# Part of the opening of a layer trunk moved between VectorE and TensorE: two tiles' modulation, and the sums of squares

## The chip, the cores and the metric

The kernel runs on one core of one Trainium2 chip. A core has a matrix engine (TensorE, PE in the profile; its weight loads are listed apart as PEld), a vector engine (VectorE, DVE), an activation engine (ScalarE, ACT), GpSimd (POOL) and SyncE (SP), which here issues the DMAs. TensorE writes into PSUM, eight banks of 128 x 512 fp32; everything else works on the on-chip memory SBUF. The metric is the device time of one execution in microseconds (us); less is better. The kernel before took 2400.89 us (median of three runs, 2396.86 to 2404.48).

## What is computed

Two layers of a trunk, each with a token mixer and a gated ConvFFN, on one sequence of 1024 tokens with 1024 features. Ahead of each sub-layer stands an RMSNorm whose result is scaled and shifted by values that come from a conditioning vector `c`:

```python
cond = jax.nn.silu(c)
for i in range(DEPTH):
    mod = (cond @ ada_w[i] + ada_b[i])[:, None, :]
    sh1, sc1, g1, sh2, sc2, g2 = jnp.split(mod, 6, axis=-1)
    h = rms_norm(x, norm_g[i, 0]) * (1.0 + sc1) + sh1
    ...   # first mixer: z = gelu(h @ w_in), u and v are its halves
```

What matters here is the first few lines for layer 0: `sh1` and `sc1` (1024 values each, the product of `cond` with 1024 x 1024 weights each), the sum of squares of each token for the norm, and then the product of `h` with the `v` half of `w_in`.

## The kernel before

Features lie on the partitions: `xT` holds x as eight tiles (d = 0 to 7) of 128 features by 1024 tokens, in two halves of 512 tokens, LO and HI. The opening works on LO. Precise products are made of three reduced ones: each operand is split into a high and a low part, and `mm3` (L277, its matmul at L280) issues high x high, high x low and low x high.

The program is a list of operations that `Plan` (L108) orders. Each has an engine, a duration as the plan supposes it, the tiles it reads and writes, and a priority `pr`; `emit` lays them out by a small model of the engines, and what comes out is the order in which each engine runs its instructions. Each engine then runs that order strictly, waiting where an operand is not there.

The opening, L992 to L1085, goes like this:

- **Fillers.** `warm` (L966) multiplies a tile of ones by itself (128 columns) into a bank that nobody reads. 14 of them stand ahead of the first real work, 10 after the sums of squares, 8 after the norm's broadcast.
- **The condition.** `c` is loaded as one row (L994), behind three of the loads of x; TensorE spreads it over 128 partitions by a product with ones (L1004, two matmuls), ScalarE takes the sigmoid (L1006), VectorE multiplies (L1007). The row, now silu(c) on every partition, stays in `raw_2` for all later dot products.
- **The norm.** For each tile ScalarE squares (L454, L1016); VectorE adds seven of the squares into `accv` (L459); TensorE sums `accv` and the last square over partitions (L1020, four one-column matmuls each, with the squares as the stationary operand). VectorE takes the root (L314 to L324), puts it on a diagonal (L368), and TensorE spreads it over the partitions (L373).
- **The modulation.** The weights of `sc1` and `sh1` for tile d lie in DRAM with outputs on the partitions (128 outputs by 1024 inputs). VectorE makes a dot product with the row of silu(c) for each: `ada_dot` (L286), 1024 elements a partition. `ada_group` (L291) adds the bias (L296) and forms the gain (L300). The same operation, `first_values` (L1034), then writes the normed tile (L1042). ScalarE makes its high part (L487), VectorE its low part (L488).
- **The weights of v** (512 KB blocks, two feature tiles each) are split by ScalarE (L500) and VectorE (L503).
- **The products.** `first_mms` (L1049) multiplies each tile with two blocks for four groups of 128 tokens, 24 matmuls a tile into all eight banks. Tile 0's come in three groups of eight: high x high, then those with tile 0's low part, then those with the weights' low part.

SyncE issues the loads in the order of the plan (`p_load`, L514): x, then for each tile its two modulation blocks, with the blocks of v between, into ten buffers that are used in turn. A buffer is loaded anew when its last reader has finished.

Of the kernel before, what the change touches and what calls it, by code (L numbers as in the profile page):

```python
# [244 lines left out]
def trunk(tc, a, pool, psum, dram):  # L245
# [45 lines left out]
    def ada_group(l, w, d=0, n=KT, nw=1):  # L291
# [4 lines left out]
        V.tensor_tensor(out=v, in0=v, in1=cols(pc("ada_b", l * 48, 48)), op=ALU.add)  # L296
# [669 lines left out]
    def warm(n, w, pr, *preds):  # L966
        for _ in range(n):
            pl.op("PE", w, lambda: PE.matmul(bank[7][:, 0:P], ones, ones, start=True, stop=True), *preds,
                  r=(onesrg,), w=(bv(7),), pr=pr)
# [24 lines left out]
    pl.op("D", 0.1, lambda: nc.sync.dma_start(condr[0:1, :], a["crow"]), w=(rv(2),), pr=SB - 31)  # L994
# [15 lines left out]
    warm(10, 0.3, SB - 29)  # L1010


    ps0, sq, sqs3 = bv(6), sqs.v[3], Seq(*sqs.v[0:3])
    for d in range(KT - 1):
        p_sum(pl, nm0, d, accv, sqs3, SB - 3)
    pl.op("S", 0.63, lambda: S.activation(sq.f, xT[:, KT - 1, LO], AF.Square), r=(xrg(KT - 1, LO),), w=(sq,), pr=SB - 3)  # L1016
    for i, x in enumerate((sq, accv)):
        def fn(i=i, x=x):
            for c in range(4):
                PE.matmul(ps0.f[:, c:c + 1], x.f[:, c * P:(c + 1) * P], ones[:, 0:1], start=i == 0 and c == 0, stop=i == 1,  # L1020
                          skip_group_check=True)
        last = pl.op("PE", 0.9, fn, r=(x,), w=(ps0,), pr=SB - 3)
    warm(10, 0.22, SB - 40, last)
# [2 lines left out]
    def chain(ops=ops):
# [2 lines left out]
    pl.op("V", 1.95, chain, r=(ps0,), w=(("small0", 0, 16),), pr=SB - 3)
    after = pl.op("V", 0.63, lambda r0=r0: nm0.diag(r0), r=(("small0", 0, 16), params), w=(accv,), pr=SB - 3)  # L1030
# [1 line left out]
    warm(8, 0.22, SB - 40, last)

    def first_values(d, raws, *preds):  # L1034
# [3 lines left out]
        def fn():  # L1038
            for m, raw in raws:
                ada_dot((m, raw.f))  # L1040
            ada_group(0, 0, d, 1, 2)
            V.scalar_tensor_tensor(out=t.f, in0=xT[:, d, LO], scalar=amul[:, d:d + 1], in1=rb.f, op0=ALU.mult, op1=ALU.mult)  # L1042
# [973 lines left out]
```

## Time and profile before

| | |
|---|---|
| median of the runs | 2400.89 us |
| profiled execution, its time | 2402.39 us |
| its span | 2400.6 us |
| TensorE busy | 2370.1 us, 99% |
| VectorE busy | 2063.9 us, 86% |
| first product of the mixer (L280) | 20.82 us |
| products run on without a gap from | 26.55 us |
| granted TensorE clock, mean | 0.994 |

The span reaches from the first to the last instruction; the time beside it is that of the same execution with what lies around it. All that the change touches lies in the first 70 us, so the views of that stretch matter: the timeline of each engine, who waits for whom, and the granted clock, a share of TensorE's full rate. A row of a timeline gives start, duration, engine, line, operation, tiles, count, and in brackets the idle time ahead of it and what ended it. Each fp32 matmul leaves two records.

### The profile page before, as it was taken

To read this page: it belongs to the slowest core of one execution; us is meant where nothing else is said; L and a number is where in the kernel's file an instruction comes from. 1 tells how busy PE (TensorE), PEld (TensorE's weight loads), DVE (VectorE), ACT (ScalarE), POOL (GpSimd) and SP (SyncE) were. 2 spreads that over 40 slices of the span, in tenths; PEclk is the share of its full clock that TensorE was granted. 3 is DMA by queue.
4 is the path that set the end of the run, shared out by engine and by line. 5 is a ranking of instruction groups with operands and counts; after the bars stand their busy time and mean duration, and the time that the engine had idled before them with its cause. 6 is when DMAs were issued, how large, how long until landed. Compare 5 with 4: busy or idle time off the path is not lost.

```text
span 2400.6 us, 32858 instructions
## 1 busy us (share of the span) xinstructions
PE 2370.1 (99%) x11358; PEld 1976.7 (82%) x11358; DVE 2063.9 (86%) x3322; ACT 1288.8 (54%) x2301; POOL 449.9 (19%) x312
## 2 busy tenths in 40 slices
PE   9999999999999999999999999999999999999998
PEld 7888887788888888888788888888888888887886
DVE  8899988988989889998988788887689988898756
ACT  4546664455555555445566666665255555544444
POOL 0222110322222221012301111111122222220121
PEclk8999999999999999999999999999999999999999
DMA  9667769720333324865301111225313333338332
GB/s 338 194 217 255 238 205 308 258 81 27 123 96 121 113 92 143 296 218 180 122 15 52 45 45 45 71 62 157 105 42 110 104 117 108 107 123 285 95 104 97
DMA packets 154827, 330.91 MB, mean 138 GB/s; under 512 B 15522, under 2 KB 34338, under 8 KB 154660
## 3 DMA queue, kind: packets, MB, share of 16 engines
q1 hardware_dynamic: 154660, 328.81, 41.8%
q8 instruction: 89, 1.46, 0.3%
q14 instruction: 78, 0.64, 0.1%
HBM read 253.77 MB, written 74.98 MB: 137 GB/s over the span
## 4 chain that ended last, share of the span: by engine, by line
PE 93%; DVE 2%; DMA 2%; issue 1%; ACT 1%; POOL 0%; SPq 0%; POOLq 0%; ACTq 0%; DVEq 0%
PE pb L280 85%; PE pb L1626 4%; PE pb L1346 1%; PE pb L1691 1%; PE pb L1711 1%; DMA h<-act 0%; PE pb L1713 0%; DVE w L503 0%; DMA xT<-vd 0%; PE pb L373 0%; DVE h L503 0%; PE pb L1684 0%; PE pb L1734 0%; DMA h<-gact 0%; DMA w<-in_down 0%
## 5 line engine op out<-in xcount | busy, mean ns | idle before, releaser
L280 PE MATMUL pb<-h,w 128*128 128x512 f32 (+1 forms) x4470 | 1038.5, 388 | 8.5 <-ACT h L500 2.9
L280 PEld LDWEIGHTS pb<-h,w 128*128 128x128 f32 x4470 | 832.5, 188 | 184.8 <-ACT h L500 4.2
L280 PE MATMUL pb<-n,w 128*128 128x512 f32 x3312 | 790.1, 391 | 1.8 <-ACT wk L735 1.0
L280 PEld LDWEIGHTS pb<-n,w 128*128 128x128 f32 x3312 | 617.6, 188 | 130.7 <-ACT wk L735 1.5
L503 POOL TENSOR_TENSOR w<-w,w 128x512 fp32r<-128x512 f32 x170 | 260.5, 1537 | 952.2 <-ACT w L500 913.9
L500 ACT ACTIVATE w<-w 128x512 fp32r<-128x512 f32 x405 | 249.8, 627 | 265.4 <-PE pb L280 162.0
L893 DVE SCALAR_TENSOR_TENSOR raw<-wk,prm,raw 128x1024 f32<-128x1024 f32 x168 | 266.3, 1594 | 7.4 <-ACT raw L889 6.3
L503 DVE TENSOR_TENSOR w<-w,w 128x512 fp32r<-128x512 f32 x235 | 169.8, 728 | 32.6 <-ACT w L500 31.7
L500 ACT ACTIVATE w<-n 128x512 fp32r<-128x512 f32 x136 | 85.8, 631 | 163.8 <-PE pb L280 151.6
L735 ACT ACTIVATE wk<-pb 128x512 f32<-128x512 f32 x160 | 94.7, 593 | 139.9 <-PE pb L280 117.7
L280 PE MATMUL pb<-w,n 128*128 128x512 f32 x612 | 144.5, 397 | 3.6 <-DVE n L488 3.6
L738 DVE TENSOR_TENSOR wk<-pb,wk 128x512 f32<-128x512 f32 x160 | 108.3, 686 | 45.5 <-PE pb L280 40.8
L280 PEld LDWEIGHTS pb<-w,n 128*128 128x128 f32 x612 | 116.5, 191 | 29.8 <-DVE n L488 4.5
L503 POOL TENSOR_TENSOR w<-raw,w 128x512 fp32r<-128x512 f32 x55 | 78.5, 1440 | 328.6 <-ACT w L500 216.9
L503 DVE TENSOR_TENSOR w<-n,w 128x512 fp32r<-128x512 f32 x136 | 101.1, 746 | 44.5 <-ACT w L500 44.1
L500 ACT ACTIVATE h<-h 128x512 fp32r<-128x512 f32 x198 | 121.8, 618 | 25.1 <-DMA h<-gact 12.8
L889 ACT ACTIVATE raw<-wk,prm 128x1024 f32<-128x1024 f32 x84 | 103.6, 1240 | 32.8 <-DVE raw L510 12.9
L280 PE MATMUL pb<-w,h 128*128 128x512 f32 x480 | 116.9, 396 | 0.0
L503 DVE TENSOR_TENSOR h<-h,h 128x512 fp32r<-128x512 f32 x150 | 110.2, 739 | 6.9 <-ACT h L500 6.9
L503 POOL TENSOR_TENSOR h<-h,h 128x512 fp32r<-128x512 f32 x48 | 67.9, 1414 | 197.9 <-ACT h L500 186.2
L280 PEld LDWEIGHTS pb<-w,h 128*128 128x128 f32 x480 | 88.1, 188 | 17.4
L442 DVE SCALAR_TENSOR_TENSOR xT<-pb,mod,xT 128x512 f32<-128x512 f32 (+1 forms) x108 | 74.4, 727 | 24.5 <-PE pb L280 24.2
(278 smaller groups left out, 2927.9 us busy)
## 6 DMA issues: line engine op xcount, KB each, us to landing
w<-in_up SPq DMA_DIRECT2D x88, 512.0 KB, 3.7
act<-raw SPq DMA_DIRECT2D x154, 256.0 KB, 2.2
h<-act SPq DMA_DIRECT2D x124, 256.0 KB, 2.8
h<-in_ada SPq DMA_DIRECT2D x45, 512.0 KB, 4.7
wk<-in_ada SPq DMA_DIRECT2D x33, 512.0 KB, 4.6
n<-in_down SPq DMA_DIRECT2D x64, 256.0 KB, 5.4
gact<-xT SPq DMA_DIRECT2D x56, 256.0 KB, 3.8
h<-gact SPq DMA_DIRECT2D x56, 256.0 KB, 3.9
```

Of the source, the lines that this page charges most:

```text
L280: PE.matmul(ps, L[i // 2], R[i % 2], start=first and i == 0 and not more, stop=last and i == 2, skip_group_check=more)
L442: V.scalar_tensor_tensor(out=xT[:, d, hs], in0=ps.f, scalar=gate(d), in1=xT[:, d, hs], op0=ALU.mult, op1=ALU.add)
L500: pl.op("S", 0.2 + 0.43 * w, lambda: S.activation(hi.r, src.f, AF.Copy), r=(src,), w=(hi,), pr=pr)
L503: lambda: e.tensor_tensor(out=lo.r, in0=src.f, in1=hi.f, op=ALU.subtract), *preds,
L735: pl.op("S", 0.6, lambda: S.activation(c.f, ps.f, AF.Copy), r=(ps,), w=(c,), pr=p(i) - 10)
L738: pl.op("V", 0.69, lambda: V.tensor_tensor(out=c.f, in0=ps.f, in1=c.f, op=ALU.add), r=(ps, c), w=(c,), pr=p(i) - 8)
L889: pl.op("S", 1.22, lambda: S.activation(y.f, wk[:, o + PADW:o + PADW + T], AF.Identity, bias=pc("conv_b", l * NUP + b), scale=cw(2)), r=(c ...
L893: pl.op("V", 1.26, lambda w=w: V.scalar_tensor_tensor(out=y.f, in0=wk[:, o + w:o + w + T], scalar=cw(w), in1=y.f, op0=ALU.mult, op1=ALU.ad ...
L1346: PE.matmul(ps.f[:, i * P:(i + 1) * P], v.f[:, i * P:(i + 1) * P], wsT[:, j, :], start=True, stop=True)
L1626: PE.matmul(ps_()[0:m, c, :], K.f[:, c * P:c * P + m], q, start=True, stop=True)
L1691: PE.matmul(b2.f[:, cs(c)], kT.f[:, cs(c)], vc(c), start=True, stop=True)
L1711: PE.matmul(b3.f[:, cs(c)], sc.f[:, cs(c)], vc(c), start=True, stop=s_ is None)
```

## The change

Four things change, all in the opening.

- **Condition.** `c` is loaded twice, ahead of x: as a column (`ccol`, 128 x 8, element k of partition p is feature 128 k + p) and as the row of before. ScalarE and VectorE make silu of the column (`csl`).
- **Squares.** ScalarE squares all eight tiles, and TensorE sums each of them as it comes: four one-column matmuls a tile, 32 in all, into one accumulation. VectorE's adds are gone. Root and diagonal become one operation of the plan, and the splits of the first two blocks of v no longer wait for a tile's values.
- **Modulation of tiles 0 and 1** (`NPE = 2`). Their weights come from a copy with inputs on the partitions (`adaf`); `pe_dots` multiplies each 128 x 128 block, as the stationary operand, by one column of `csl`: eight matmuls for each of the two columns of a tile, into one column of bank 7 (tile 0) or 5 (tile 1). `ada_group` then reads the sums from PSUM. Tiles 2 to 7 stay with VectorE.
- **Fillers.** 7 in place of 14 ahead of the squares, 4 in place of 10 behind them, 4 in place of 8 behind the norm's broadcast; they write bank 3 instead of 7.

```diff
@@ ada_group
-    def ada_group(l, w, d=0, n=KT, nw=1):
+    def ada_group(l, w, d=0, n=KT, nw=1, ps=None):
...
-        V.tensor_tensor(out=v, in0=v, in1=cols(pc("ada_b", l * 48, 48)), op=ALU.add)
+        src = v if ps is None else ps.rearrange("p (w d) -> p w d", d=n)
+        V.tensor_tensor(out=v, in0=src, in1=cols(pc("ada_b", l * 48, 48)), op=ALU.add)
@@ the opening
-    pl.op("D", 0.1, lambda: nc.sync.dma_start(condr[0:1, :], a["crow"]), w=(rv(2),), pr=SB - 31)
+    cc, csig, csl = (cct[:, i * KT:i * KT + KT] for i in range(3))
+    ccrg = ("cc", 0, 1)
+
+    def load_cond():
+        nc.sync.dma_start(cc, a["ccol"])
+        nc.sync.dma_start(condr[0:1, :], a["crow"])
+    pl.op("D", 0.2, load_cond, w=(ccrg, rv(2)), pr=SB - 32)
+    pl.op("S", 0.25, lambda: S.activation(csig, cc, AF.Sigmoid), w=(ccrg,), pr=SB - 32)
+    pl.op("V", 0.17, lambda: V.tensor_tensor(out=csl, in0=cc, in1=csig, op=ALU.mult), w=(ccrg,), pr=SB - 32)
...
-    warm(10, 0.3, SB - 29)
+    warm(3, 0.3, SB - 29)
...
-    ps0, sq, sqs3 = bv(6), sqs.v[3], Seq(*sqs.v[0:3])
-    for d in range(KT - 1):
-        p_sum(pl, nm0, d, accv, sqs3, SB - 3)
-    pl.op("S", 0.63, lambda: S.activation(sq.f, xT[:, KT - 1, LO], AF.Square), r=(xrg(KT - 1, LO),), w=(sq,), pr=SB - 3)
-    for i, x in enumerate((sq, accv)):
-        def fn(i=i, x=x):
+    ps0, psd = bv(6), (bv(7), bv(5))
+    nm0.acc = accv.f
+    for d in range(KT):
+        q = sqs.next()
+        pl.op("S", 0.6, lambda d=d, q=q: S.activation(q.f, xT[:, d, LO], AF.Square), r=(xrg(d, LO),), w=(q,), pr=SB - 25 + d)
+
+        def fn(d=d, q=q):
             for c in range(4):
-                PE.matmul(ps0.f[:, c:c + 1], x.f[:, c * P:(c + 1) * P], ones[:, 0:1], start=i == 0 and c == 0, stop=i == 1,
-                          skip_group_check=True)
-        last = pl.op("PE", 0.9, fn, r=(x,), w=(ps0,), pr=SB - 3)
-    warm(10, 0.22, SB - 40, last)
+                PE.matmul(ps0.f[:, c:c + 1], q.f[:, c * P:(c + 1) * P], ones[:, 0:1], start=d == 0 and c == 0,
+                          stop=d == KT - 1, skip_group_check=True)
+        last = pl.op("PE", 0.7, fn, r=(q, onesrg), w=(ps0,), pr=SB - 25 + d)
+    warm(4, 0.22, SB - 40, last)
...
-    warm(8, 0.22, SB - 40, last)
+    warm(4, 0.22, SB - 40, last)
+
+    def pe_dots(d, raws):
+
+        for m, raw in raws:
+            def fn(raw=raw, col=m // KT):
+                for k in range(KT):
+                    PE.matmul(psd[d].f[:, col:col + 1], raw.f[:, k * P:k * P + P], csl[:, k:k + 1], start=k == 0, stop=k == KT - 1)
+            pl.op("PE", 1.2, fn, r=(raw, ccrg), w=(psd[d],), pr=SB - 2.5 + d)
@@ first_values
-            ada_group(0, 0, d, 1, 2)
+            ada_group(0, 0, d, 1, 2, psd[d].f[:, 0:2] if d < NPE else None)
@@ the loop over tiles and blocks
-            after = p_split(pl, x, *vset[p, q], "V", SB + nw - 1.4 if nw < 8 else SB + 9 + nw, ys[-1])
+            after = p_split(pl, x, *vset[p, q], "V", SB + nw - 1.4 if nw < 8 else SB + 9 + nw, ys[-1] if nw > 1 else None)
...
-            p_load(pl, x, a["ada"][0, m], pr)
-        if d == 0:
-            p_dot(*raws.pop(0), SB, after)
+            p_load(pl, x, a["adaf"][m // KT, d] if d < NPE else a["ada"][0, m], pr)
+        if d < NPE:
+            pe_dots(d, raws)
+            raws = []
@@ _lay_out
+    first = stat(f["ada_w"][0][:, :2 * D])
+    out["adaf"] = np.stack([first[0:NPE], first[KT:KT + NPE]])
+    out["ccol"] = cols(f["c"])
```

TensorE's order in the opening is the first place of which the prediction speaks. `pb_75` to `pb_82` are the banks 0 to 7, `h_...` and `w_...` are buffers with a version number, and each row is an instruction as the program has it (two records each in the profile). Before, from the start:

```order
L968 MATMUL pb_82<-ones 128x128 x14
L1004 MATMUL pb_79<-raw_67,ones 128x512
L1004 MATMUL pb_80<-raw_67,ones 128x512
L1020 MATMUL pb_81<-ones,wk 128x1 x8
L968 MATMUL pb_82<-ones 128x128 x10
L373 MATMUL pb_81<-wk,ones 128x512
L968 MATMUL pb_82<-ones 128x128 x8
L280 MATMUL pb_75<-w_177,n_203 128x512
L280 MATMUL pb_76<-w_177,n_203 128x512
```

After, from the start; the first product, `L281 MATMUL pb_75<-w_223,n_238 128x512`, stands right behind the last row:

```order
L970 MATMUL pb_78<-ones 128x128 x5
L1015 MATMUL pb_79<-raw_67,ones 128x512
L1015 MATMUL pb_80<-raw_67,ones 128x512
L970 MATMUL pb_78<-ones 128x128 x2
L1032 MATMUL pb_81<-ones,wk 128x1 x32
L970 MATMUL pb_78<-ones 128x128 x4
L1051 MATMUL pb_82<-cc,h_116 128x1 x8
L1051 MATMUL pb_82<-cc,h_136 128x1 x8
L375 MATMUL pb_81<-wk,ones 128x512
L970 MATMUL pb_78<-ones 128x128 x4
L1051 MATMUL pb_80<-cc,h_158 128x1 x8
L1051 MATMUL pb_80<-cc,h_177 128x1 x8
```

The squares' sums grew from 8 to 32 rows, and two groups of 16 one-column matmuls stand between them and the first product, one ahead of the norm's broadcast (L375, before L373) and one behind it.

VectorE's order from the last step of the root on is the second place; `mod` holds the modulation, `amul` the gains, L1042 or L1062 writes a normed tile, L488 or L490 its low part, L503 or L505 splits a block of v. Before:

```order
L324 SCALAR_TENSOR_TENSOR small<-small 128x4
L368 TENSOR_TENSOR wk<-prm,small 128x512
L288 SCALAR_TENSOR_TENSOR h_119,mod<-h_119,raw_67 128x1024
L288 SCALAR_TENSOR_TENSOR h_128,mod<-h_128,raw_67 128x1024
L296 TENSOR_TENSOR mod<-mod,prm 128x2
L300 SCALAR_TENSOR_TENSOR amul<-mod,prm 128x1
L1042 SCALAR_TENSOR_TENSOR xT<-xT,amul,pb_81 128x512
L503 TENSOR_TENSOR w_200<-h_135,w_167 128x1024
L503 TENSOR_TENSOR w_205<-h_143,w_177 128x1024
L288 SCALAR_TENSOR_TENSOR h_163,mod<-h_163,raw_67 128x1024
L288 SCALAR_TENSOR_TENSOR h_173,mod<-h_173,raw_67 128x1024
```

After:

```order
L326 SCALAR_TENSOR_TENSOR small<-small 128x4
L370 TENSOR_TENSOR wk<-prm,small 128x512
L505 TENSOR_TENSOR w_201<-h_148,w_189 128x1024
L298 TENSOR_TENSOR mod<-pb_82,prm 128x2
L302 SCALAR_TENSOR_TENSOR amul<-mod,prm 128x1
L1062 SCALAR_TENSOR_TENSOR xT<-xT,amul,pb_81 128x512
L505 TENSOR_TENSOR w_236<-h_191,w_223 128x1024
L298 TENSOR_TENSOR mod<-pb_80,prm 128x2
L302 SCALAR_TENSOR_TENSOR amul<-mod,prm 128x1
L1062 SCALAR_TENSOR_TENSOR xT<-xT,amul,h_234 128x512
L490 SCALAR_TENSOR_TENSOR n_246<-xT,mod,n_238 128x512
```

The four dot products of tiles 0 and 1 (L288) are gone, the bias of these tiles is added from banks 7 and 5, and a split stands ahead of tile 0's bias. Tile 0's low part (`n_246`, before `n_209`) still stands behind tile 1's values.

SyncE's first loads are the third place. Before:

```order
L996 DMA xT<-in_x 128x2x512 x3
L994 DMA raw_67<-in_crow 1x1024
L996 DMA xT<-in_x 128x512 x2
L514 DMA h_119<-in_ada 128x1024
L998 DMA prm<-in_params 128x256
L514 DMA h_128<-in_ada 128x1024
L514 DMA h_135<-in_wv 128x1024
L514 DMA h_143<-in_wv 128x1024
L514 DMA h_163<-in_ada 128x1024
```

After:

```order
L1001 DMA cc<-in_ccol 128x8
L1002 DMA raw_67<-in_crow 1x1024
L1007 DMA xT<-in_x 128x2x512 x3
L1007 DMA xT<-in_x 128x512 x2
L516 DMA h_116<-in_adaf 128x1024
L1009 DMA prm<-in_params 128x256
L516 DMA h_136<-in_adaf 128x1024
L516 DMA h_148<-in_wv 128x1024
L516 DMA h_158<-in_adaf 128x1024
L516 DMA h_177<-in_adaf 128x1024
```

Column and row now stand ahead of x. The second block of v, `h_143` before, has moved behind tile 1's two modulation blocks.

More of the change, by code (lines that the diff above doesn't have):

```diff
@@ L37 @@
 NPLAIN = 2
+NPE = 2
 NV_ADA = (16, 3)
@@ L260, in trunk @@
     small = pool.tile([P, 64], F32, name="small")
-    pool.tile([P, 24], F32, name="gap")
+    cct = pool.tile([P, 3 * KT], F32, name="cc")
     bank = [psum.tile([P, 512], F32, name=f"pb{i}") for i in range(8)]
@@ L967, in warm @@
         for _ in range(n):
-            pl.op("PE", w, lambda: PE.matmul(bank[7][:, 0:P], ones, ones, start=True, stop=True), *preds,
-                  r=(onesrg,), w=(bv(7),), pr=pr)
+            pl.op("PE", w, lambda: PE.matmul(bank[3][:, 0:P], ones, ones, start=True, stop=True), *preds,
+                  r=(onesrg,), w=(bv(3),), pr=pr)
     def p_dot(m, x, pr, *preds, cond=rv(2)):
@@ L1008, in trunk, with chain @@
               r=(b, xrg(i, HI)), w=(c,), pr=SB - 2.5)
[L1010 to L1018 removed]
+    warm(3, 0.3, SB - 29)
[5 more added lines that the diff above has]
+        def fn(d=d, q=q):
             for c in range(4):
[L1020 to L1023 removed]
+                PE.matmul(ps0.f[:, c:c + 1], q.f[:, c * P:(c + 1) * P], ones[:, 0:1], start=d == 0 and c == 0,
+                          stop=d == KT - 1, skip_group_check=True)
+        last = pl.op("PE", 0.7, fn, r=(q, onesrg), w=(ps0,), pr=SB - 25 + d)
+    warm(4, 0.22, SB - 40, last)
     r0, ops = small_ops(ps0.f[:, 0:4], 4, 1.0 / D)
[L1026 removed]
+    def chain(ops=ops, r0=r0):
         for f in ops:
             f()
[L1029 to L1030 removed]
+        nm0.diag(r0)
+    after = pl.op("V", 2.6, chain, r=(ps0, params), w=(("small0", 0, 16), accv), pr=SB - 3)
     last = pl.op("PE", 0.86, lambda: nm0.bcast(ps0.f), r=(accv,), w=(ps0,), pr=SB - 3)
[L1032 removed]
+    warm(4, 0.22, SB - 40, last)
[5 more added lines that the diff above has]
+            pl.op("PE", 1.2, fn, r=(raw, ccrg), w=(psd[d],), pr=SB - 2.5 + d)
     def first_values(d, raws, *preds):
@@ L1040, in fn @@
                 ada_dot((m, raw.f))
-            ada_group(0, 0, d, 1, 2)
+            ada_group(0, 0, d, 1, 2, psd[d].f[:, 0:2] if d < NPE else None)
             V.scalar_tensor_tensor(out=t.f, in0=xT[:, d, LO], scalar=amul[:, d:d + 1], in1=rb.f, op0=ALU.mult, op1=ALU.mult)
         raw = [x for _, x in raws]
-        x = pl.op("V", 1.42 + 1.23 * len(raws), fn, *preds, r=(*raw, rv(2), xrg(d, LO), rb, params),
+        x = pl.op("V", 1.42 + 1.23 * len(raws), fn, *preds, r=(*raw, rv(2) if raw else psd[d], xrg(d, LO), rb, params),
                   w=(*raw, t, modrg(0, 0, d), modrg(0, 1, d), ("amul", d, d + 1)), pr=pr, port=True)
```

2 lines of the change are left out of this document (1 added, 1 removed).

## The prediction

> **What bounds the kernel now.** I read the head of the page first, then who TensorE waits for in the first 110 us, then TensorE's timeline from the start, and last the granted clock in that stretch.
>
> ```profile
> span 2400.6 us, 32858 instructions
> PE 2370.1 (99%) x11358; PEld 1976.7 (82%) x11358; DVE 2063.9 (86%) x3322; ACT 1288.8 (54%) x2301; POOL 449.9 (19%) x312
> ```
> ```profile
> PE pb L280 <- DVE n L488: 3.6, 1, 3.6
> PE pb L968 <- DVE ones L992: 1.1, 1, 1.1
> PE pb L1004 <- DMA raw<-in_crow: 0.9, 1, 0.9
> ```
> TensorE (PE) is busy for 99% of the span. Up to 110 us it waits three times, 5.6 us together, and the only long wait is the 3.6 us before a product of the first value tiles. So a change at the start is worth what it moves the moment from which TensorE's products run on without a gap, and what it changes in their rate. The timeline of TensorE alone shows this opening (start, duration, line, tiles, count; an fp32 matmul leaves two records, which I call passes):
>
> ```profile
> 1.05 5.29 PE L968 MATMUL pb<-ones 128*128 128x128 f32 x28 [1.05 <-DVE ones L992]
> 7.28 2.64 PE L1004 MATMUL pb<-raw,ones 1*128 1x512 f32 x4 [0.94 <-DMA raw<-in_crow]
> 9.86 3.57 PE L1020 MATMUL pb<-ones,wk 128*128 128x1 f32 x16
> 13.29 4.61 PE L968 MATMUL pb<-ones 128*128 128x128 f32 x20
> 17.70 1.53 PE L373 MATMUL pb<-wk,ones 128*128 128x512 f32 x2
> 19.06 1.95 PE L968 MATMUL pb<-ones 128*128 128x128 f32 x16
> 20.82 2.10 PE L280 MATMUL pb<-w,n 128*128 128x512 f32 x8
> 26.55 48.79 PE L280 MATMUL pb<-w,n 128*128 128x512 f32 x202 [3.62 <-DVE n L488]
> ```
> Before 20.82 us no product of the mixer runs: there are fillers (L968), the row broadcast (L1004), the sums of squares (L1020), and the broadcast of the norm (L373). Eight products run at 20.82, then nothing until 26.55. What stands in these gaps is VectorE:
>
> ```profile
> 13.47 0.16 DVE L314 TENSOR_SCALAR small<-pb 128x4 f32<-128x4 f32 x1 [0.50 <-PE pb L1020]
> 15.45 0.69 DVE L368 TENSOR_TENSOR wk<-prm,small 128x512 f32<-128x512 f32 x1
> ...
> 19.27 0.75 DVE L1042 SCALAR_TENSOR_TENSOR xT<-xT,amul,pb 128x512 f32<-128x512 f32 x1 [0.45 <-PE pb L373]
> 20.05 0.72 ACT L487 ACTIVATE n<-xT,mod 128x512 fp32r<-128x512 f32 x1 [0.83 <-DVE xT L1042]
> ```
> ```profile
> 19.93 2.35 DVE w L503 x2
> 22.28 2.30 DVE h L288 x4
> ...
> 24.61 0.17 DVE mod L296
> ...
> 24.80 0.17 DVE amul L300
> ...
> 25.08 0.75 DVE xT L1042
> 25.83 0.67 DVE n L488
> ```
> (The first fence is the timeline, the second the chain of waits, which VectorE holds here.) The norm's root takes VectorE from 13.47 to 16.14; tile 0's two dot products follow, and tile 0's values at 19.27, with their high part on ScalarE at 20.05. Then come two splits of weights (2.35 us), tile 1's two dots (2.30), its bias, gain and values, and tile 0's low part, which is what releases TensorE at 26.55. The second thing to read is the clock, in stretches that I cut where the granted clock changes (5.05, 8.46, 18.70, 25.53 and 32.35 us, whole multiples of 3.41 us apart; columns: busy time of PE, weight loads, DVE, ACT, POOL, then clock):
>
> ```profile
> 8.46:11.87 3.41, 3.41 (x12) 2.01 (x10) 2.19 (x4) 3.38 (x6) 0.00 (x0) 0.50 1.03 402
> 11.87:15.28 3.41, 3.41 (x17) 3.41 (x17) 2.60 (x12) 2.28 (x3) 0.00 (x0) 0.50 1.03 412
> 15.28:18.70 3.42, 3.42 (x15) 2.90 (x14) 3.32 (x8) 0.64 (x2) 0.00 (x0) 0.50 1.02 407
> 25.53:28.94 3.41, 2.39 (x6) 1.91 (x7) 3.41 (x5) 1.78 (x2) 0.00 (x0) 0.50 0.95 353
> 28.94:32.35 3.41, 3.41 (x10) 2.64 (x9) 3.31 (x8) 1.31 (x2) 0.00 (x0) 0.50 1.06 327
> 32.35:35.77 3.42, 3.42 (x17) 2.81 (x16) 3.31 (x8) 0.36 (x1) 0.00 (x0) 1.00 0.96 374
> ```
> The clock is half from 8.46 to 18.70 and from 25.53 to 32.35. The second half-rate stretch lies on products: 26.55 to 32.35 is 5.8 us in which half the work gets done, a loss of 2.9 us. The first lies on the squares' sums:
>
> ```profile
> L968 PE MATMUL pb<-ones 128*128 128x128 f32 x9 | 2.3, 437 | 0.0
> L1020 PE MATMUL pb<-ones,wk 128*128 128x1 f32 x8 | 1.8, 352 | 0.0
> ```
> From 11.87 to 15.28 TensorE was busy without a break, 1.8 us on one-column matmuls and the rest on 128-column fillers, and yet the clock stayed at half. In 15.28 to 18.70, with wide matmuls alone, it rose. I conclude that **matmuls with one moving column do not count as enough work for full clock**. (The 1.00 that the views show before 5.05 is no reading: fillers there last 433 ns, as in the half-rate stretch, where full rate has 275.)
>
> **The change, part by part.**
>
> *Prices.* At half clock a one-column pass costs 3.50 / 16 = 0.22 us, at full clock 0.79 / 8 = 0.10 (I take 0.11):
>
> ```profile
> 9.93 3.50 PE pb L1020 x16
> ...
> 82.13 0.79 PE pb L363 x8
> ```
> A filler pass costs 4.61 / 20 = 0.23 at half and 1.95 / 16 = 0.12 at full. A 512-column fp32 pass costs 1.7 / 2 = 0.85 at half; half of that, 0.43, is my estimate for full:
>
> ```profile
> L1004 PE MATMUL pb<-raw,ones 1*128 1x512 f32 x2 | 1.7, 942 | 0.0
> ```
> *Loads.* The column and the row of the condition now go ahead of x, some 0.45 us of issue each:
>
> ```profile
> 0.74 1.47 SPq L996 DMA_DIRECT2D xT<-in_x  x3
> 2.24 0.37 SPq L994 DMA_DIRECT2D raw<-in_crow  x1
> 4.78 1.15 ACT L454 ACTIVATE wk<-xT 128x512 f32<-128x512 f32 x2 [2.77 <-DMA xT<-in_x]
> ```
> ```profile
> act<-raw SPq DMA_DIRECT2D x154, 256.0 KB, 2.2
> h<-in_ada SPq DMA_DIRECT2D x45, 512.0 KB, 4.7
> ```
> x comes 0.8 us later, 5.6 instead of 4.78, and so do the weights behind it. The row need no longer queue behind three tiles of x: issued at 1.2, it lands near 3.4 with the 2.2 us that the page's 256 KB stores take. The column is 128 pieces of 32 bytes, which no row shows; between nothing and the 5.0 us that the row took (2.24 to 7.24), I take 2.2. Even 5 us would hide: its first reader is ScalarE's sigmoid, queued ahead of the squares, which wait for x until 5.6 anyway, and TensorE needs the column only at its dots. If cover failed, 0.6 us. The table load that ScalarE saves (1.28 us) was already off the path.
>
> *Squares.* VectorE loses its adds; TensorE has 32 matmuls, 64 passes, where it had 8. At half clock this is 64 x 0.22 = 14.1 us. They start after 10 filler passes from 1.05 (to 3.4), four row-broadcast passes at 0.85 (to 6.8) and four fillers (to 7.7); the first square is ready at 6.2, so TensorE and no longer ScalarE sets the pace. End 21.8, against 13.43.
>
> *Dots.* Eight matmuls for each column of 128, 16 a tile, 32 passes, 32 x 0.22 = 7.0 us a tile. TensorE's order holds tile 0's dots ahead of the norm's broadcast and tile 1's ahead of the first product, so all of it is on the path: fillers 1.8 (23.6), dots 7.0 (30.6), broadcast 1.7 (32.3), fillers 1.8 (34.1), dots 7.0 (**41.1**). VectorE's root (2.7 us, ready at 24.5) and tile 0's values (32.3 + 0.75 + 0.72 = 33.8) hide beside. The weights have landed long before. So the first product starts at 41.1 in place of 20.82: **+20.3 us**.
>
> *What is released.* The 3.62 us gap goes: tile 1's values need only 1.9 us on VectorE after the dots (bias, gain, values, low part: 0.16, 0.16, 0.75, 0.75 and gaps), by 43.0 (rows of the chain above), while eight products at half clock last until 44.5. **-3.6 us**. The half-rate stretch stays, because the dots keep the clock low: from 41.1 between one and two stretches of 3.41 us pass before it rises, 1.7 to 3.4 us lost, I take 2.5 against 2.9. **-0.4 us**.
>
> *Who waits next.* VectorE does the dots of tiles 2 to 7 as before, and is near its limit:
>
> ```profile
> 42.96 0.75 DVE L1042 SCALAR_TENSOR_TENSOR xT<-xT,amul,h 128x512 f32<-128x512 f32 x1
> ...
> 59.71 0.75 DVE L1042 SCALAR_TENSOR_TENSOR xT<-xT,amul,h 128x512 f32<-128x512 f32 x1
> ```
> These are the values of tiles 4 and 7: 16.75 / 3 = 5.6 us a tile, where TensorE takes 24 products of 0.227 (from the row at 26.55: 202 in 48.79 less 2.9), 5.45 us. After 43.0 VectorE makes a split and tile 1's low part (1.9 us), then tile 2's dots, and has tile 2's values at about 48.3; TensorE wants them at 41.1 + 2.5 + 48 x 0.227 = 54.5. That lead of 6 us loses 0.2 a tile: it holds. SyncE's queue is held longer: the reload of tile 0's two buffers (tile 3's weights) waits for the dots until 30.6, tile 1's (half of tile 4's) until 41.1, and every later load stands behind. With the page's 4.7 us to land they are there at 46, and VectorE wants tile 4's at about 56.
>
> *Not shown in the trace*: eight passes in a row that accumulate onto one PSUM column. Products at L280 already put three passes in a row on one bank without a gap, so I take nothing; the other end is that each pass lasts its whole recorded 352 ns, 0.13 us more for each of the 64 dot passes, +8.5 us. No reason speaks for a gain, since the weight load sets the pace.
>
> **Sum** against the profiled run: 2402.39 + 20.3 - 3.6 - 0.4 = 2418.7. That run is 1.5 us above the median of 2400.89, so the forecast is **2417**. Behind 70 us TensorE has no wait for a long time, so nothing gives it back.
>
> **Rivals.**
> - *Full clock through the dots* (not slower). If the stream of one-column matmuls holds or raises the clock, squares end with ScalarE's last one: 5.6 + ten activations of 0.6 = 11.6, plus 0.8 for the last four sums, 12.4; fillers 1.0, dots 3.5, broadcast 0.9, fillers 1.0, dots 3.5, first product at 22.3 (+1.5). Tile 1's low parts come at 24.2, eight products last until 24.1, so the gap goes (-3.5), and so does the half-rate stretch (-2.9). Sum -4.9: 2396 beside the median. For it: TensorE stands idle nowhere after 3.4 us. Against it: the stretch 11.87 to 15.28. What decides is when the clock rises: if only at the end of the squares, 21.8, the first product comes at 21.8 + 1.0 + 3.5 + 0.9 + 1.0 + 3.5 = 31.7, and the sum is +10.9 - 3.5 - 2.9 = +4.5: 2405 beside the median, still too little to be told from no change. Chance 0.13, the late rise in it.
>  [...]
> - *A lift in the middle.* Broadcast and fillers after it are 3.5 us of wide matmuls; if they fall on one window, tile 1's dots run at full: 32 x 0.11 = 3.5 us less, 2413.5. Chance 0.12.
> - *Serial accumulation*: +8.5, 2425.5. Chance 0.05.
> - *The change does not do what it says*: the orders show the dots gone from VectorE and on TensorE, so no chance of its own.
>
> **How the numbers follow.** The forecast has 0.66 (2413 to 2421, from 1.7 to 3.4 us of half clock, and from where the stretches lie). The remaining 0.04 is for a gain that I do not see. The range, 2408 to 2424, takes in forecast and lift and leaves out 0.2. A measurement of this kernel can tell about 0.3% from no change, 7.2 us, so "same" ends at 2408.1: slower 0.82 (forecast, lift, serial), same 0.14 (full clock), faster 0.04.
>
> **What would show it.** In the changed profile: the squares' 64 passes at 0.22 us each ending near 22 with granted clock 0.5 (wrong if 0.11 and clock 1.0); each dot group about 7 us long; the first product near 41; no wait of TensorE behind it; the clock full by 48. The forecast is wrong if the granted clock is 1.0 anywhere between 8 and 30 us, or if the first value products come before 35.

## The result, and the profile after

The changed kernel takes 2416.52 us (median of five runs, 2412.65 to 2425.48) beside 2401.85 us for the kernel before (five runs, 2396.86 to 2404.48). The ratio is 1.0068, with a 95% interval of 1.0054 to 1.0082: **14.7 us slower**, where 2417 us was forecast. The profiled execution is the highest of the five, 2425.48 us; 23.1 us of span lie between it and the profiled execution of before.

The head of its page, to be read beside that of before:

```profile
span 2423.7 us, 33002 instructions
PE 2394.0 (99%) x11436; PEld 1999.1 (82%) x11436; DVE 2058.5 (85%) x3309; ACT 1286.5 (53%) x2301; POOL 450.5 (19%) x312
```

TensorE is as full as it was (99%), and its busy time grew by 23.9 us, which is as much as the span did. VectorE has 5.4 us less to do; nothing came of that. TensorE's timeline from the start shows where the work stands:

```profile
1.05 2.50 PE L970 MATMUL pb<-ones 128*128 128x128 f32 x10 [1.05 <-DVE ones L994]
3.48 3.78 PE L1015 MATMUL pb<-raw,ones 1*128 1x512 f32 x4
7.19 1.22 PE L970 MATMUL pb<-ones 128*128 128x128 f32 x4
8.21 13.65 PE L1032 MATMUL pb<-ones,wk 128*128 128x1 f32 x64
21.72 2.05 PE L970 MATMUL pb<-ones 128*128 128x128 f32 x8
23.57 6.83 PE L1051 MATMUL pb<-cc,h 128*128 128x1 f32 x32
30.25 2.06 PE L375 MATMUL pb<-wk,ones 128*128 128x512 f32 x2
32.10 1.91 PE L970 MATMUL pb<-ones 128*128 128x128 f32 x8
33.81 6.83 PE L1051 MATMUL pb<-cc,h 128*128 128x1 f32 x32
40.49 49.81 PE L281 MATMUL pb<-w,n 128*128 128x512 f32 x208
```

The 64 passes for the squares last 13.65 us, 0.213 us each; the two groups of dots 6.83 us each, again 0.213 a pass; all behind one another, and the first product starts at 40.49, before at 20.82. No row has a bracket behind the first one, so TensorE stands idle nowhere. The list of its waits up to 140 us has no row but that one.

VectorE's timeline has the other side: it now stands idle ahead of each step that needs TensorE, 12.43, 4.72 and 6.44 us (the brackets).

```profile
21.89 0.16 DVE L316 TENSOR_SCALAR small<-pb 128x4 f32<-128x4 f32 x1 [12.43 <-PE pb L1032]
...
30.43 0.16 DVE L298 TENSOR_TENSOR mod<-pb,prm 128x2 f32<-128x2 f32 x1 [4.72 <-PE pb L1051]
...
40.67 0.16 DVE L298 TENSOR_TENSOR mod<-pb,prm 128x2 f32<-128x2 f32 x1 [6.44 <-PE pb L1051]
```

The clock behind the first product, in stretches of 4 us (columns as in the prediction; the counts of PE are the ones to read):

```profile
40.00:44.00 4.00, 4.00 (x11) 3.28 (x12) 3.18 (x6) 2.08 (x3) 0.00 (x0) 1.00 0.49 144
44.00:48.00 4.00, 4.00 (x16) 3.21 (x15) 3.90 (x9) 0.69 (x2) 0.00 (x0) 1.00 0.64 190
48.00:52.00 4.00, 4.00 (x19) 3.34 (x18) 3.90 (x8) 1.53 (x2) 0.00 (x0) 1.00 0.97 325
```

11 matmul passes, then 16, then 19. The granted clock is printed as 1.00 in all three, but that is no reading: the trace records its first change of the clock, a rise, at 45.6 us, and the pace tells that it was half until some point between 44 and 48. By the last row's pace the 7.51 us from 40.49 to 48.00 hold 35.7 products; 27 less the 2.3 passes of dots that still ran in the first row were done, so 11 products of 0.21 us, 2.3 us, were lost.

To see how much of the time was lost in the opening alone, I use eight passes that stand behind the same 240 product passes in all the kernels of this study: the sums of squares of the other half. Before, in TensorE's timeline:

```profile
81.97 0.95 PE L363 MATMUL pb<-ones,wk 128*128 128x1 f32 x8
```

And the same passes in the timeline of after:

```profile
97.39 0.94 PE L365 MATMUL pb<-ones,wk 128*128 128x1 f32 x8
```

15.4 us of the 23.1 us are there by then. The other 7.7 us came later, in the part of the program that the change doesn't touch. A second profile of the same kernel (below) has 2.4 us in place of them.

### The profile page after: what moved, and what is told of

The parts are those of the page before. It is cut to its first block, busy times and chain, and to the rows that moved or that the text cites. A ratio compares the mean times of both kernels' runs of the same rounds, so it can differ in the third digit from the quotient of the medians.

```text
span 2423.7 us, 33002 instructions
## 1 busy us (share of the span) xinstructions
PE 2394.0 (99%) x11436; PEld 1999.1 (82%) x11436; DVE 2058.5 (85%) x3309; ACT 1286.5 (53%) x2301; POOL 450.5 (19%) x312
## 4 chain that ended last, share of the span: by engine, by line
PE 92%; DMA 3%; DVE 2%; issue 2%; ACT 1%; POOL 0%; SPq 0%; POOLq 0%; DVEq 0%; ACTq 0%
PE pb L281 83%; PE pb L1647 4%; PE pb L1367 1%; DMA h<-gact 1%; DMA xT<-vd 1%; PE pb L1032 1%; PE pb L1712 1%; PE pb L1732 1%; DVE h L505 1%; PE pb L1051 1%; PE pb L1734 0%; DMA h<-act 0%; DVE w L505 0%; PE pb L375 0%; DMA n<-in_wo 0%
## 5 line engine op out<-in xcount | busy, mean ns | idle before, releaser
L281 PE MATMUL pb<-h,w 128*128 128x512 f32 (+1 forms) x4470 | 1042.4, 389 | 9.9 <-DVE w L505 3.4
L281 PEld LDWEIGHTS pb<-h,w 128*128 128x128 f32 x4470 | 834.8, 188 | 187.9 <-DVE w L505 5.0
L281 PE MATMUL pb<-n,w 128*128 128x512 f32 x3312 | 790.0, 392 | 1.8 <-ACT wk L737 1.0
L281 PEld LDWEIGHTS pb<-n,w 128*128 128x128 f32 x3312 | 617.8, 188 | 130.2 <-ACT wk L737 1.5
L505 POOL TENSOR_TENSOR w<-w,w 128x512 fp32r<-128x512 f32 x170 | 262.3, 1548 | 955.8 <-ACT w L502 910.4
L505 DVE TENSOR_TENSOR w<-w,w 128x512 fp32r<-128x512 f32 x235 | 169.2, 726 | 31.6 <-ACT w L502 30.8
L281 PE MATMUL pb<-w,n 128*128 128x512 f32 x612 | 143.9, 396 | 0.0
L505 POOL TENSOR_TENSOR w<-raw,w 128x512 fp32r<-128x512 f32 x55 | 78.0, 1430 | 345.8 <-ACT w L502 292.9
L505 DVE TENSOR_TENSOR w<-n,w 128x512 fp32r<-128x512 f32 x136 | 101.1, 746 | 47.6 <-ACT w L502 47.5
L281 PEld LDWEIGHTS pb<-w,n 128*128 128x128 f32 x612 | 116.5, 191 | 25.7 <-issue 1.0
L891 ACT ACTIVATE raw<-wk,prm 128x1024 f32<-128x1024 f32 x84 | 103.6, 1240 | 33.4 <-DVE raw L512 12.7
L281 PE MATMUL pb<-w,h 128*128 128x512 f32 x480 | 116.9, 396 | 0.0
L505 DVE TENSOR_TENSOR h<-h,h 128x512 fp32r<-128x512 f32 x150 | 109.4, 733 | 8.2 <-ACT h L502 8.2
L505 POOL TENSOR_TENSOR h<-h,h 128x512 fp32r<-128x512 f32 x48 | 67.8, 1412 | 200.3 <-ACT h L502 188.6
L281 PEld LDWEIGHTS pb<-w,h 128*128 128x128 f32 x480 | 88.1, 188 | 17.4
```

What stands on the lines that cost most here:

```text
L281: PE.matmul(ps, L[i // 2], R[i % 2], start=first and i == 0 and not more, stop=last and i == 2, skip_group_check=more)
L505: lambda: e.tensor_tensor(out=lo.r, in0=src.f, in1=hi.f, op=ALU.subtract), *preds,
L891: pl.op("S", 1.22, lambda: S.activation(y.f, wk[:, o + PADW:o + PADW + T], AF.Identity, bias=pc("conv_b", l * NUP + b), scale=cw(2)), r=(c ...
```

## The experiments

The theory: one-column matmuls leave the clock at half however densely they stand, so 0.213 us a pass in the opening is the half-clock price of a weight load, and 0.11, an estimate from the 0.79 us that eight such passes took before at 82.13, would be the full one. The rival: the price of such a pass is what it is (a fixed cost of a new stationary operand, of the accumulation in one column, or of fp32), and the clock merely happened to be low. The second question is which of the two parts, squares or dots, costs the time. The times of before among the runs that were made together were 2400.95 to 2402.15 (medians of 12 to 17).

**Only one part at a time.** First the squares as before (VectorE adds seven, TensorE does 16 passes), the dots on TensorE:

```diff
-    for d in range(KT):
-        q = sqs.next()
-        pl.op("S", 0.6, lambda d=d, q=q: S.activation(q.f, xT[:, d, LO], AF.Square), r=(xrg(d, LO),), w=(q,), pr=SB - 25 + d)
...
+    sq, sqs3 = sqs.v[3], Seq(*sqs.v[0:3])
+    for d in range(KT - 1):
+        p_sum(pl, nm0, d, accv, sqs3, SB - 3)
+    pl.op("S", 0.63, lambda: S.activation(sq.f, xT[:, KT - 1, LO], AF.Square), r=(xrg(KT - 1, LO),), w=(sq,), pr=SB - 3)
+    for i, x in enumerate((sq, accv)):
...
```

> Squares are added by VectorE again (16 passes on TensorE in place of 64); the dots of tiles 0 and 1 stay on TensorE. Theory (the loss is one-column passes at half clock, 0.215 us each, all ahead of the first product): tile 0's first weights land near 11 us, from there 80 passes take 17.2 us, the fillers and the norm's broadcast 3.7, the value and its high part 1.5, so the first product comes near 33 in place of 40.5, and the time falls by about 7 us to 2409. Rival (the dots alone make the whole loss, since they stand between norm and products): first product still near 40, time 2416. Granted clock half until the products.

Then the dots back on VectorE, the squares on TensorE:

```diff
-NPE = 2
+NPE = 0
```

> All dots on VectorE again, the squares' 64 passes stay on TensorE. Theory: squares end near 23.5 (13.8 us of passes and 3.5 of the row's broadcast from 6.2), root until 26.2, split and two dots until 30, first product near 31.7, no long gap behind it because tile 0's 24 products run at half clock; time about 2409. With the run before this, the two parts' savings add to less than the whole 15 us, because in either alone VectorE or a load takes over as the last wait. Rival (squares cost nothing, they run beside the loads): first product at 21 to 23, time 2402.

This one didn't run: with no tile on TensorE, the copy of the weights with inputs on the partitions had no elements, and the program failed to load. The next keeps the copy, which then nothing reads.

```diff
-NPE = 2
+NPE = 0
...
-    out["adaf"] = np.stack([first[0:NPE], first[KT:KT + NPE]])
+    out["adaf"] = np.stack([first[0:2], first[KT:KT + 2]])
```

> All dots on VectorE again, the squares' 64 passes stay on TensorE (the first build of this could not be loaded, since an input had no elements; the input is now kept and not read). Theory: squares end near 23.5 (13.8 us of one-column passes and 3.5 of the row's broadcast, from 6.2), root until 26.2, split and two dots until 30, first product near 31.7, no long gap behind it; time about 2409. Rival (squares cost nothing, they run beside the loads): first product at 21 to 23, time 2402.

Squares as before: 2412.13 us (2411.33 to 2414.12), ratio 1.0043, 1.0029 to 1.0056. In TensorE's timeline the dots of tile 0 moved in between the sums, and the first product stands at 33.40:

```profile
10.47 3.57 PE L1052 MATMUL pb<-cc,h 128*128 128x1 f32 x16
...
22.58 6.83 PE L1052 MATMUL pb<-cc,h 128*128 128x1 f32 x32
...
33.40 54.69 PE L281 MATMUL pb<-w,n 128*128 128x512 f32 x240 [0.39 <-ACT n L489]
```

Dots as before: 2409.99 us (2408.46 to 2411.01), ratio 1.0036, 1.0023 to 1.005; first product at 31.36:

```profile
5.55 6.99 PE L1032 MATMUL pb<-ones,wk 128*128 128x1 f32 x32 [1.15 <-ACT wk L1028]
...
31.36 56.31 PE L281 MATMUL pb<-w,n 128*128 128x512 f32 x240 [1.87 <-ACT n L489]
```

The passes cost the same in both, 0.21 to 0.22 us. The first products came near where they were expected (33 and 31.7); the time of the first kernel was 3 us over the 2409 expected. Both are slower than before by 8 to 10 us, clear of the noise: **both parts cost**.

Their losses don't simply add. By the eight passes of the other half, the openings lost 6.0 us (87.93) and 5.5 us (87.51) against before, together 11.5, where both parts lost 15.4 in the profile above. The first product comes 12.6 and 10.5 us later than before, together 23.1, where both parts make 19.7: in either alone TensorE still waits ahead of it, 2.8 and 3.9 us by their timelines, in the changed kernel only the 1.05 us that all have at the start. From the first product to the eight passes it is 61.2 us before, 54.5 and 56.2 in these two, 56.9 in the changed kernel. So 6.6 and 5.0 us come back, and 4.3 in the changed kernel: 3.6 in each for the gap, and the rest because less of the way is run at half clock (the first of the two starts its products at full clock, with 13 and 15 passes in two stretches of 3 us from 33.4 on).

**The same passes, but 128 columns wide.** Every one-column matmul now streams 128 columns: the squares against all of the tile of ones, the dots against the condition's column broadcast to 128; one of the 128 equal results is read. The order of every engine is that of the changed kernel, instruction by instruction, and so are the number of passes and the weights that they load.

```diff
-                PE.matmul(ps0.f[:, c:c + 1], q.f[:, c * P:(c + 1) * P], ones[:, 0:1], start=d == 0 and c == 0,
+                PE.matmul(ps0.f[:, c * P:(c + 1) * P], q.f[:, c * P:(c + 1) * P], ones, start=d == 0 and c == 0,
...
-                    PE.matmul(psd[d].f[:, col:col + 1], raw.f[:, k * P:k * P + P], csl[:, k:k + 1], start=k == 0, stop=k == KT - 1)
+                    PE.matmul(psd[d].f[:, col * P:col * P + P], raw.f[:, k * P:k * P + P], csl[:, k:k + 1].to_broadcast([P, P]), start=k == 0, stop=k == KT - 1)
```

> The same weights in the same order, but each of the 96 matmuls streams 128 columns (the squares against all of the ones, the dots against the condition's column repeated) where it streamed one; only one column of the result is read. Theory (the weight load sets the pace, and one moving column is too little work for full clock): at half clock a pass costs 0.23 in place of 0.215, but the clock rises to full between 10.6 and 14 us, passes then cost 0.12; squares end near 18, first product near 28, no half clock behind; about 2402, 14 us less than the change. Rival (the passes cost 0.22 us whatever the clock, or the clock stays low for another reason): 128 times the columns save nothing, first product at 41 or later, time 2416 or more.

2402.4 us (2399.2 to 2408.79, 11 runs), ratio 1.0004, 0.9995 to 1.0013: the whole loss is gone, by streaming 128 times as many columns. TensorE's timeline:

```profile
8.21 8.69 PE L1032 MATMUL pb<-ones,wk 128*128 128x128 f32 x64
17.63 3.74 PE L1051 MATMUL pb<-cc,h 128*128 128x128 f32 x32
...
26.45 55.10 PE L281 MATMUL pb<-w,n 128*128 128x512 f32 x240
```

The squares last 8.69 us in place of 13.65, each group of dots 3.74 in place of 6.83 (0.117 us a pass), and the first product starts at 26.45. Two stretches of 2.8 us show when it happens:

```profile
8.20:11.00 2.80, 2.80 (x16) 2.80 (x15) 0.69 (x1) 1.26 (x3) 0.00 (x0) 1.00 1.05 402
11.40:14.20 2.80, 2.80 (x28) 2.80 (x27) 0.00 (x0) 2.05 (x4) 0.00 (x0) 1.00 1.02 407
```

And the same stretches in the changed kernel:

```profile
8.20:11.00 2.80, 2.80 (x15) 2.80 (x15) 0.69 (x1) 1.17 (x3) 0.00 (x0) 1.00 1.05 400
11.40:14.20 2.80, 2.80 (x15) 2.80 (x15) 0.00 (x0) 1.26 (x2) 0.00 (x0) 1.00 1.02 405
```

15 passes and 16 in the first, then 15 and 28. In the first stretch a pass cost the same with one column as with 128, and the weight loads (PEld) filled all of the 2.80 us in both, so the moving side wasn't what set its time; from about 11.3 us, some 3.1 us after the first sum, the wide kernel ran at nearly twice the pace (28 beside 15), the narrow one never in its 13.65 us. **The theory is shown for these two kernels; the rival falls**, for nothing but the width differs (and with it how many equal results are written).

**Can a longer run of wide matmuls ahead of the dots do it?** 24 fillers in place of 4 behind the squares; dots with one column.

```diff
-    warm(4, 0.22, SB - 40, last)
+    warm(24, 0.22, SB - 40, last)
```

> 20 more fillers (128 columns wide) between the squares and tile 0's dots. Theory: the fillers, 48 passes in all, raise the clock to full within 3.4 to 6.8 us (so they take about 8 us, not 11), tile 0's one-column dots then begin at 0.11 us a pass and the clock falls back to half within them or shortly behind, by tile 1's dots, which take 6.8 us as before. Time about 2420. Rival (it is a high clock once reached that lasts as long as TensorE stands busy): both groups of dots take 3.5 us, clock full throughout, time about 2413.

A single run: 2419.57 us. The planner now put the norm's broadcast ahead of both groups of dots, so that these are one row. TensorE's timeline:

```profile
21.72 6.97 PE L970 MATMUL pb<-ones 128*128 128x128 f32 x48
...
30.27 9.50 PE L1051 MATMUL pb<-cc,h 128*128 128x1 f32 x64
39.64 50.64 PE L281 MATMUL pb<-w,n 128*128 128x512 f32 x211
```

And its stretches of 3.41 us each:

```profile
21.41:24.83 3.42, 3.42 (x18) 3.42 (x18) 2.59 (x12) 0.00 (x0) 0.00 (x0) 1.00 0.15 55
24.83:28.24 3.41, 3.41 (x33) 3.41 (x32) 2.01 (x2) 0.00 (x0) 0.00 (x0) 1.00 0.00 0
...
31.65:35.07 3.42, 3.42 (x32) 3.42 (x31) 1.05 (x3) 0.00 (x0) 0.00 (x0) 0.96 0.53 153
35.07:38.48 3.41, 3.41 (x18) 3.41 (x17) 0.01 (x1) 2.15 (x3) 0.00 (x0) 0.50 0.85 312
```

The fillers raise the clock (18 passes, then 33, in equal stretches). The dots run at full clock at first, 32 passes in 3.42 us. But they are the only work on TensorE from 30.27 on, and from 35.07 the granted clock is 0.50 and the pace 18 a stretch. So one-column passes not only failed to raise the clock in the changed kernel (13.65 us), here it **fell** to 0.50 under a gapless stream of them, within 4.8 us of its start. The dots gained 4.2 us (9.50 in place of twice 6.83) and the broadcast 1.0 (1.02 us in place of 2.06), and the fillers took 4.9 more: the other half's passes start at 96.69, 0.7 us before those of the changed kernel.

**How wide is wide enough?** 64 columns in place of 128, at the same two lines.

```diff
+                PE.matmul(ps0.f[:, c * P:c * P + 64], q.f[:, c * P:(c + 1) * P], ones[:, 0:64], start=d == 0 and c == 0,
...
+                    PE.matmul(psd[d].f[:, col * P:col * P + 64], raw.f[:, k * P:k * P + P], csl[:, k:k + 1].to_broadcast([P, 64]), start=k == 0, stop=k == KT - 1)
```

> As the run with 128 columns, but each of the 96 matmuls streams 64. A pass is still as long as its weight load, with columns moving half of that time at half clock. Theory (what counts is the share of time in which columns move; 0.70 of a window, before 28.94 in the first kernel, did not raise the clock): the clock stays at half, first product near 40, time 2416. Rival (any width from some tens of columns on counts as busy): clock full by 14, first product near 27, time 2402.

A single run: 2409.2 us, between the two, and neither theory had that. TensorE's timeline:

```profile
8.20 13.76 PE L1032 MATMUL pb<-ones,wk 128*128 128x64 f32 x64
...
23.56 4.41 PE L1051 MATMUL pb<-cc,h 128*128 128x64 f32 x32
...
29.61 3.68 PE L1051 MATMUL pb<-cc,h 128*128 128x64 f32 x32
33.10 55.09 PE L281 MATMUL pb<-w,n 128*128 128x512 f32 x240
```

The squares run at half clock for all of their 13.76 us, like one column. The clock rises in the first group of dots, behind eight 128-column fillers (32 passes in 4.41 us), and the second group runs at full (3.68) with no drop behind it. So 64 columns didn't raise the clock in 13.76 us, and it did not fall in 3.7 us of them; the second is weaker, since wide matmuls stand close before and behind that group. What widths between 64 and 128 do, and whether raising and holding go alike, no run shows.

**The changed kernel once more**, unchanged, for a second profile.

> The changed kernel once more, for a second profile. Theory (the 7.7 us by which its first profiled run was later at the end than behind the opening belong to that run): opening the same within 1 us, first product at 40 to 41, time 2413 to 2419. Rival (they belong to the change): again about 2425.

2416.45 us, span 2414.6. The other half's passes start at 93.53, 11.6 us after those of before, and not 15.4, and the first product comes before the 40 to 41 expected. TensorE's timeline shows why:

```profile
33.81 3.72 PE L1051 MATMUL pb<-cc,h 128*128 128x1 f32 x32
37.39 52.90 PE L281 MATMUL pb<-w,n 128*128 128x512 f32 x225
```

So do its stretches:

```profile
34.24:37.65 3.41, 3.41 (x31) 3.41 (x31) 0.08 (x1) 1.04 (x2) 0.00 (x0) 0.96 0.70 219
37.65:41.06 3.41, 3.41 (x9) 2.72 (x10) 3.26 (x6) 2.24 (x3) 0.00 (x0) 0.54 0.93 366
```

Tile 1's dots took 3.72 us: here the clock did rise in the broadcast and the fillers ahead of them, the dots ran at full (31 passes in 3.41 us), and at their end it fell again, so that the first products ran for one stretch at half (9 passes, granted clock 0.54). That is the second rival of the prediction, in one profile of two. Its condition, that the wide matmuls "fall on one window" (one step of 3.41 us between two places where the clock was seen to change), can be read too. In the first profile the recorded changes stand at 45.62, 472.28, 475.70, 1199.32 and 1202.74 us, which is 125, 1, 212 and 1 times 3.413 us apart, whole multiples as in the prediction, and these steps lie differently against the program in the two profiles. Here the first rise is recorded at 34.0, and the step ahead of it, 30.6 to 34.0, holds broadcast and fillers, and dots only in its last 0.2 us. In the first profile, with its rise at 45.6, the steps are 28.6 to 32.0 and 32.0 to 35.4, and each holds over 1.5 us of one-column dots. The two profiles fit; they are no more than two.

The rest of this profile's 14.0 us of span, 2.4 us, came later, in place of 7.7.

**Two versions meant to beat both.** From the wide kernel: two tiles' squares added by VectorE before TensorE sums them (32 passes), fillers from the first microsecond until the sums, the condition's row and its broadcast behind the sums.

```diff
+        if d % 2 == 0:
+            qq = q
+            continue
+        pl.op("V", 0.68, lambda q=q, qq=qq: V.tensor_tensor(out=qq.f, in0=qq.f, in1=q.f, op=ALU.add), r=(q,), w=(qq,), pr=SB - 25 + d)
...
-    warm(3, 0.3, SB - 29)
+    warm(10, 0.2, SB - 29)
...
-            pl.op("PE", 1.2, fn, r=(raw, ccrg), w=(psd[d],), pr=SB - 2.5 + d)
+            pl.op("PE", 1.9, fn, summed, r=(raw, ccrg), w=(psd[d],), pr=SB - 2.5 + d)
```

> 128 columns as in that run, and the opening arranged for a full clock: VectorE adds the squares in pairs (32 passes in place of 64), 34 filler passes run without a break from 1 us until the first pair is there, none behind; the row's broadcast comes behind the norm's, the column is loaded ahead of x and the row behind it, and dots follow the sums. Theory: clock full by 4.5 to 8, sums end at 11.5, tile 0's dots at 15.2, broadcasts at 17.9, first product near 21.6 in place of 26.45, no gap and no half clock behind: 4.8 us less than with 128 columns alone, 2397.5, some 0.2% faster than before. Rival (loads set the opening now: tile 1's weights and the second block of v land too late): first product at 25 or later, or gaps behind it, 2401 to 2403.

2408.86 us (2404.97 to 2414.13), ratio 1.003, 1.0018 to 1.0041: slower. The first product starts at 23.98, and the other half's passes at 78.51, 3.5 us before those of before. By the medians (7.1 us over before) some 10 us were lost behind them. TensorE's waits from 80 to 300 us:

```profile
PE pb L281 <- ACT w L502: 3.2, 1, 3.2
PE pb L1375 <- DVE xT L740: 2.7, 1, 2.7
```

The 1.9 us that I had given the planner for a group of dots moved operations far behind the opening, and VectorE and ScalarE are late there. The second version is the same with 1.2 us there, which leaves the order behind the opening as it is in the changed kernel:

```diff
-            pl.op("PE", 1.9, fn, summed, r=(raw, ccrg), w=(psd[d],), pr=SB - 2.5 + d)
+            pl.op("PE", 1.2, fn, summed, r=(raw, ccrg), w=(psd[d],), pr=SB - 2.5 + d)
```

> The opening of the arranged run before (pairs, fillers from 1 us, 128 columns), but with the plan's supposed durations set so that all engines have the same order as in the changed kernel from the eight first products' outputs on; in the run before, the order of some thousand later operations had changed too. Theory (the 10 us that the arranged run lost behind 80 us belong to the changed order there): opening as in that run, the sums of the second half's squares (8 one-column passes) at 78 to 79.5 in place of 82.1 before, the rest as long as in the run with 128 columns, time 2397 to 2399. Rival (VectorE, busy for nearly all of 90 to 260 us, is the bound there, so that a TensorE that comes earlier only waits): time 2401 to 2403, with new waits of TensorE for VectorE of 3 us or more between 80 and 260 us.

2402.27 us (2400.07 to 2407.38, 11 runs), ratio 1.0007, 0.9998 to 1.0016: no better than before. Its timeline of TensorE:

```profile
1.05 6.97 PE L970 MATMUL pb<-ones 128*128 128x128 f32 x34 [1.05 <-DVE ones L994]
7.86 1.95 PE L1030 MATMUL pb<-ones,wk 128*128 128x128 f32 x16
...
22.81 55.10 PE L281 MATMUL pb<-w,n 128*128 128x512 f32 x240
77.75 0.95 PE L365 MATMUL pb<-ones,wk 128*128 128x1 f32 x8
```

The opening is 4.2 us shorter than before's (77.75 beside 81.97), and at the end nothing is left of it. In this profile the clock is at half from 447.7 to 454.5, behind a wait of 3.0 us, as TensorE's timeline has it:

```profile
448.24 8.11 PE L281 MATMUL pb<-h,w 128*128 128x512 f32 x22 [2.96 <-DVE xT L444]
```

The stretch in question:

```profile
447.70:454.50 6.80, 6.26 (x15) 4.95 (x16) 6.80 (x10) 3.57 (x7) 3.38 (x3) 0.51 0.43 133
```

15 passes in 6.8 us, where the wide kernel has 32 in the same stretch: 3.4 us. The profile of before has the same wait at the same place, 2.6 us long, and no drop behind it:

```profile
450.23 5.94 PE L280 MATMUL pb<-h,w 128*128 128x512 f32 x25 [2.62 <-DVE xT L442]
```

The two rows start with the same product, so of the 4.2 us only 2.0 were left by then; waits for ScalarE and VectorE, this one and shorter ones, had taken the rest, and the stretch at half clock took what was left. The rival's waits of 3 us or more for VectorE between 80 and 260 us were not there. That is one profile; how often the drop comes in this version's runs is not known (the last section says what goes with it). No version here beats the kernel before.

## Why the prediction was right

- **Clock.** "Matmuls with one moving column do not count as enough work for full clock": shown for this kernel by the wide one, and once more by the 24 fillers. The sign "granted clock 1.0 anywhere between 8 and 30 us" can't be taken from the printed 1.00 of these stretches, since no change is recorded before 45.6 us; 0.213 us a pass is the half pace, beside 0.116 (3.72 / 32) where the dots ran at full in the second profile. The wide kernel's squares came to the full pace some 3.1 us after the first of them; the one-column passes stayed at half for 13.65 us without a gap.
- **Squares.** 64 passes of 0.22 us to 21.8; measured 0.213, to 21.86.
- **Dots.** 7.0 us a group, all on the path; measured 6.83, and 3.72 for the second group in the second profile. First product at 41.1; measured 40.49, and 37.39.
- **The gap.** 3.62 us gone, and no wait in its place: so it was, and so it is in each half of the change alone.
- **Half clock behind the first product.** 2.5 us forecast, about 2.3 counted; full by 48 in both.
- **Sum.** 20.3 - 3.6 - 0.4 = 16.3 forecast. In the first profile the first product came 19.7 us later, 3.6 went with the gap, and the opening lost 15.4 in all, so that 0.7 is left for the half-clock stretch in place of 0.4. The medians differ by 14.7. That the forecast meets the median within half a microsecond is luck: two profiles of the changed kernel differ by 3.8 us in the opening and by 5.3 behind it.
- **VectorE's lead and the reloads** hid, as argued: TensorE has no wait up to 140 us.
- **The lift in the middle** had a chance of 0.12; it happened in one profile of two, which is too few to give its chance, and is worth 3.8 us (15.4 - 11.6; 3.5 forecast). So the forecast was made for one of two cases that both occur. (The chances for slower, 0.66, 0.12 and 0.05, add up to 0.83, where 0.82 is written.) Serial accumulation cost nothing here: the dots, eight matmuls in a row onto one column, took 0.213 us a pass, and so did the squares, whose matmuls go to four columns in turn.
- **What was not foreseen** is the 7.7 us that the first profile lost later, and that 4 us won in the opening are not seen in the total. Parts of both are half-clock stretches behind waits (in the last version 2.96 us of wait, then half clock from 447.7 to 454.5 us; in the first profile 2.95 us, then half from 472.28 to 475.70), and small waits for ScalarE and VectorE.

## What to carry to other kernels

In this kernel a chain of matrix-vector products or column sums on TensorE had one weight load a pass (64 of each for the squares), and in the first profile, with one moving column, all of it ran at half clock, 0.213 us a pass, and the first products behind it too (about 2.3 us lost). Streaming 128 equal columns in place of one cost nothing (16 passes in 2.8 us beside 15, both at half) and brought a pass of the dots to 0.117 us. Whether another kernel's chain does the same is for its own trace to show. What moves to an idle stretch of the bounding engine still has to be shorter there than the wait that it takes away: 27.3 us of one-column passes stand where 3.6 had been, for a gap of 3.62 us. In a planned program, change the planned durations with care: a number that was closer to the measured one moved work far behind the place and cost more than the edit won.
